# The input projection in seven block products instead of eight, in two causal halves

## The chip, the cores and the metric

The kernel runs on one core of a Trainium2 chip, in fp32 throughout. The metric is the device time of one execution in microseconds (us), lower is better. TensorE (PE) does the matrix products, VectorE (DVE) and ScalarE (ACT) the elementwise work, SyncE (SP) issues nearly all DMAs. A matmul writes to PSUM, of which there are eight banks of 128 x 512 fp32.

## The reference

One step of a hybrid decoder layer, for 2048 prompt tokens and 8 single sample tokens, model width 1024. The input projection has 11,264 columns: three attention groups (q, k, v of 512 columns each; dilations 1, 4, 16), an attention gate, the HGRN q, f, i and gate (1024 each), and two merge gates (1024 each).

```python
h = rms_norm(x, norm_w)
q, k, v = [cols(h, w_in, base + j * ATT_W, ATT_W) ...]      # three groups
o, lse = dilated_attn_prompt(q, k, v, win, dil, slopes[g])  # 129 keys a query
att = sum_g softmax_g(lse) * o ;  att = att * silu(cols(h, w_in, OFF_ATT_GATE, ATT_W))
ho, s_new = hgrn2_chunked(hq, hk, hi, logf, s0)             # causal, a state per head
ho = rms_norm(ho, hg_norm_w) * silu(cols(h, w_in, OFF_HG_GATE, HG_VW))
merged = ga * (att @ w_att_proj) + gb * (ho @ w_hg_proj)
y = x + merged @ w_out                                      # then a final rms_norm
```

The sample tokens attend to three caches of keys and values (8 heads of 64, 8 sequences) and update a stored HGRN state of 8 sequences x 8 heads x 128 x 128. Keys, values and states are outputs too.

## The kernel before

**Products.** The normalized input stays in SBUF, transposed, split into a high and a low fp32r part (`hh`, `hl`), in five token chunks of 512, 512, 512, 256 and 264 (the last holds the 8 sample tokens). A weight block is split the same way. A product takes three passes: high x high, high x low, low x high. `nat` makes 128 tokens x 256 columns (V of attention, i of HGRN) with 24 matmuls of 256 columns. `proj_T` makes 128 columns x all tokens, with the weights as the stationary side: per column block and chunk 24 matmuls, at L320, L321 and L322. Each chunk has a PSUM tile of its own (`pp`, two or three banks in rotation), so an eviction lies beside the next chunk's matmuls.

**Stages**, in the order of TensorE: `nat_block` over ten column blocks; attention, 12 pairs of a head pair j and a group g, where the projection of one pair stands beside the scores, the transposes of the probabilities and the value products of the pair before (`att_proj`, `att_side`); `combine` with the decode attention (`samp_score`, `samp_softmax`, `samp_av`) and gates between; HGRN, eight heads, with the projections of f, q and gate and merge gates; the sample HGRN (`samp_hg`, L891 to L905, and `samp_hg_end`) with merge gates between the heads; a branch `tc.If` (L977) that an exact version is behind; the last merge gate; and the final products. Scores of attention go through VectorE (bias and row maximum), ScalarE (exponential), TensorE (transposes) and a copy, block after block.

**What sets the order.** The kernel's code is put in order by a scheduler with priorities: `tc.high_priority` raises weight loads and splits. Every engine executes its queue in order. Pools of buffers decide how early a load may start.

The lines that make one product, as they stand before:

```python
for t0, npr, n in chunks:
    ci = chunk_of(t0)[0]
    ps = ps_proj()
    for k in range(KT):
        TE.matmul(ps[:, 0:n], hi[:, k], hh[ci][:, k], start=(k == 0), stop=False)
        TE.matmul(ps[:, 0:n], hi[:, k], hl[ci][:, k], start=False, stop=False)
        TE.matmul(ps[:, 0:n], lo[:, k], hh[ci][:, k], start=False, stop=(k == KT - 1))
    evac(ci, t0, npr, ps)
```

## Time and profile before

| | before |
|---|---|
| time, median of 3 runs | 3129.62 us (3129.3 to 3129.8) |
| span of the profiled execution | 3129.9 us |
| PE busy | 3077.8 us, 98% |
| DVE busy | 1215.5 us, 39% |
| ACT busy | 1090.5 us, 35% |
| matmuls | 19836 |
| DMA | 282.89 MB, mean 90 GB/s |

Busy time is the time in which an engine has an instruction under way. Matmuls overlap, and their ends are modelled, so that a TensorE that is held up a little between two matmuls still counts as busy. Start-to-start times of equal matmuls show the rate. Where a stage is looked at, its length, the work in it and the granted clock stand in one row of the windows view.

### The profile page before, as it was taken

The numbers are of one execution on the slowest core, as the hardware profiler recorded it, in microseconds if no ns is written. First come the engines' busy times: TensorE is split into PE (matmuls) and PEld (weight loads), VectorE is DVE, ScalarE is ACT, GpSimd is POOL, SyncE is SP. The second block draws the span as 40 slices with busy tenths as digits, with TensorE's granted clock in tenths as the row PEclk, the third lists the DMA queues.
The fourth block names the chain that finished last, engine by engine and source line by source line (L and its number), as shares of the span: only waits on it lengthen the run. The fifth ranks groups of instructions, "written<-read, shape, count | busy, mean of one in ns | idle before, by whom it ended". The sixth has DMA issues, their size and how long they took to land. (4 is left out here: it accounts for less than half of the span.)

```text
span 3129.9 us, 49890 instructions
## 1 busy us (share of the span) xinstructions
PE 3077.8 (98%) x19836; PEld 2607.1 (83%) x19836; DVE 1215.5 (39%) x3445; ACT 1090.5 (35%) x2506; POOL 3.1 (0%) x9
## 2 busy tenths in 40 slices
PE   8999999999999999999999999999999989899999
PEld 8999999777777777777878688888888868899987
DVE  5311110332332332333665055555555523634443
ACT  4311110333333333335333166655555431311231
POOL 0000000000000000000000000000000000000000
PEclk9999999999999999999999999999999989999999
DMA  5323211111111111111784311111111263744542
GB/s 167 98 89 105 79 58 41 43 45 55 42 45 55 43 45 56 42 45 64 231 275 157 121 50 42 45 41 44 40 49 48 69 183 116 223 143 134 158 149 80
DMA packets 326244, 282.89 MB, mean 90 GB/s; under 512 B 21161, under 2 KB 284026, under 8 KB 325474
## 3 DMA queue, kind: packets, MB, share of 16 engines
q1 hardware_dynamic: 325378, 277.72, 28.6%
q8 instruction: 157, 2.57, 0.3%
q0 software_dynamic: 336, 1.05, 0.1%
q10 hardware_dynamic: 288, 0.85, 0.1%
q14 instruction: 85, 0.70, 0.1%
HBM read 179.12 MB, written 100.94 MB: 89 GB/s over the span
## 5 line engine op out<-in xcount | busy, mean ns | idle before, releaser
L320 PE MATMUL pp<-hh,wh 128*128 128x512 f32 (+2 forms) x2680 | 956.6, 357 | 5.1 <-ACT gm L526 4.4
L321 PE MATMUL pp<-hl,wh 128*128 128x512 f32 (+2 forms) x2680 | 947.6, 354 | 0.0
L322 PE MATMUL pp<-hh,wl 128*128 128x512 f32 (+2 forms) x2680 | 946.6, 353 | 0.0
L320 PEld LDWEIGHTS pp<-hh,wh 128*128 128x128 f32 x2680 | 506.6, 189 | 86.2 <-issue 9.9
L321 PEld LDWEIGHTS pp<-hl,wh 128*128 128x128 f32 x2680 | 507.7, 189 | 73.0 <-issue 8.3
L322 PEld LDWEIGHTS pp<-hh,wl 128*128 128x128 f32 x2680 | 505.5, 189 | 75.0 <-issue 7.9
L207 PE MATMUL pp<-wnh,hh 128*128 128x256 f32 x1296 | 369.7, 285 | 0.5 <-ACT hh L232 0.5
L209 PE MATMUL pp<-wnh,hl 128*128 128x256 f32 x1296 | 367.5, 284 | 0.0
L208 PE MATMUL pp<-wnl,hh 128*128 128x256 f32 x1296 | 367.4, 283 | 0.0
L207 PEld LDWEIGHTS pp<-wnh,hh 128*128 128x128 f32 x1296 | 247.6, 191 | 4.8 <-issue 3.5
L209 PEld LDWEIGHTS pp<-wnh,hl 128*128 128x128 f32 x1296 | 247.5, 191 | 0.7 <-DVE hl L235 0.2
L208 PEld LDWEIGHTS pp<-wnl,hh 128*128 128x128 f32 x1296 | 247.6, 191 | 0.4
L415 ACT ACTIVATE sc<-sc,stg 128x256 f32<-128x256 f32 (+1 forms) x384 | 175.6, 458 | 115.7 <-DVE stg L413 115.5
L176 ACT ACTIVATE wh<-wr 128x512 fp32r<-128x512 f32 x134 | 77.4, 624 | 360.3 <-PE pp L321 356.7
L413 DVE CUSTOM_DVE_ANT_0 sc<-px,bt 128x256 f32<-128x256 f32 (+1 forms) x384 | 131.0, 364 | 176.1 <-PE px L411 146.4
L177 DVE TENSOR_TENSOR wl<-wr,wh 128x512 fp32r<-128x512 f32 x134 | 86.8, 688 | 220.8 <-ACT wh L176 219.9
L411 PE MATMUL px<-kT,qT 64*128 64x256 f32 (+1 forms) x768 | 164.7, 379 | 0.0
L264 DVE COPY vst<-pp 128x256 f32<-128x256 f32 x80 | 33.9, 424 | 281.7 <-PE pp L209 281.6
L264 ACT COPY vst<-pp 128x256 f32<-128x256 f32 x80 | 29.7, 372 | 320.7 <-PE pp L209 302.1
L423 PEld LDWEIGHTS px<-cm,sc 128*128 128x128 f32 x600 | 66.0, 140 | 85.4 <-ACT sc L415 38.6
L423 PE MATMUL px<-cm,sc 128*128 128x128 f32 x600 | 130.4, 297 | 6.1 <-ACT sc L415 5.7
L176 ACT ACTIVATE th<-ra 128x256 fp32r<-128x256 f32 (+1 forms) x148 | 57.9, 417 | 221.8 <-PE pp L1025 156.9
(363 smaller groups left out, 4405.8 us busy)
## 6 DMA issues: line engine op xcount, KB each, us to landing
wr<-in_w_in SPq DMA_DIRECT2D x136, 256.0 KB
natt<-stg SPq DMA_DIRECT2D x48, 264.0 KB
na<-natt SPq DMA_DIRECT2D x48, 264.0 KB
vscr<-vst SPq DMA_DIRECT2D x48, 256.0 KB
vt<-vscr SPq DMA_DIRECT2D x48, 256.0 KB
g<-gm SPq DMA_DIRECT2D x45, 256.0 KB
wnr<-in_w_in SPq DMA_DIRECT2D x40, 256.0 KB
xt<-in_x_prompt SPq DMA_DIRECT2D x16, 512.0 KB
```

Source lines behind the costliest of these rows:

```text
L176: A.activation(out=hi, in_=raw, func=AF.Copy)
L177: V.tensor_tensor(out=lo, in0=raw, in1=hi.bitcast(F32), op=ALU.subtract)
L207: TE.matmul(ps[0:m, 0:256], lhs_hi[:, k], wt[0][:, k], start=(k == 0), stop=False)
L208: TE.matmul(ps[0:m, 0:256], lhs_hi[:, k], wt[1][:, k], start=False, stop=False)
L209: TE.matmul(ps[0:m, 0:256], lhs_lo[:, k], wt[0][:, k], start=False, stop=(k == KT - 1))
L320: TE.matmul(ps[:, 0:n], hi[:, k], hh[ci][:, k], start=(k == 0), stop=False)
L321: TE.matmul(ps[:, 0:n], hi[:, k], hl[ci][:, k], start=False, stop=False)
L322: TE.matmul(ps[:, 0:n], lo[:, k], hh[ci][:, k], start=False, stop=(k == KT - 1))
L411: TE.matmul(spss[hx][:, 0:W], qT[hs, blk * P:(blk + 1) * P], kT[hs, k0:k0 + W], start=True, stop=True)
L413: V.tensor_tensor_reduce(out=sc[:, hx, 0:W], in0=spss[hx][:, 0:W], in1=bt[:, hx, 256 - W:256], scale=1.0, scalar=3e38, op0=ALU.add, op1=AL ...
L415: A.activation(out=sc[:, hx, 0:W], in_=sc[:, hx, 0:W], func=AF.Exp, scale=-1.0, bias=stg[:, u, 128 + hx:129 + hx], accum_out=stg[:, u, 130 ...
L423: TE.transpose(pt[:, hx * W + w * P:hx * W + (w + 1) * P], sc[:, hx, w * P:(w + 1) * P], ident)
```

## The change

One level of Strassen's scheme (in Winograd's form) on the input projection. A product of 1024 tokens (a causal half p) with a pair of column blocks is split in two along the contraction (512 + 512), the tokens (r = 0, 1; 512 each) and the pair. Seven block products, in the order `A11, A12, S2, S3, S1, A22, S4`, take the place of eight; each still has three passes.

- `make_H` makes the seven combinations of the input, each split in high and low, for one half of the tokens; there is one set of tiles, written again for the second half (`hscr` keeps the normalized input meanwhile).
- `w_combos` makes the seven of the weights, per pair and half, with eleven operations of VectorE and seven of ScalarE.
- `t_pair` (the matmuls at L362, L364, L365) replaces `proj_T`: three accumulators `pa`, `pb`, `pc`, one bank each; `pa` is reused four times a chunk after a copy by ScalarE (`keep_c`), `pc` twice. The chunks of a block are 256 and 260 tokens in the first half (with four sample tokens) and 512 in the second (`SETS`).
- `nat_block` (L308, L310, L311) does the same with two banks each.
- Natural products, attention, combine and HGRN run for the first half, then for the second; keys go through DRAM (`kscr`), the HGRN state stays in SBUF (`carry_s`). Dilation 16 works on 64-row pieces.
- The decode attention stands in the first half's combine stage. The sample HGRN stands between the halves, without projections between its heads. The flag is read and the branch taken after the second half, and one merge pair stands behind the branch.

```diff
+HALF = T // 2
+SW = 512 + NS // 2
+SETS = (((0, 256), (256, 260)), ((0, 512),))
+ORDER = ("A11", "A12", "S2", "S3", "S1", "A22", "S4")
...
+    def make_H(a11, a12, a21, a22, cs):
+        def put_h(s, src):
+            split_w(src, Hh[s][:, :, cs], Hl[s][:, :, cs])
+
+        put_h("A11", a11)
+        put_h("A12", a12)
+        V.tensor_tensor(out=a11, in0=a11, in1=a21, op=ALU.subtract)
+        V.tensor_tensor(out=a21, in0=a21, in1=a22, op=ALU.add)
+        put_h("A22", a22)
+        V.tensor_tensor(out=a22, in0=a22, in1=a11, op=ALU.subtract)
+        put_h("S2", a22)
+        put_h("S3", a11)
+        put_h("S1", a21)
+        V.tensor_tensor(out=a12, in0=a12, in1=a22, op=ALU.subtract)
+        put_h("S4", a12)
...
+            def prod(ps, i, ks, first=False):
+                hi, lo = Hh[ORDER[i]], Hl[ORDER[i]]
+                wh, wl = W[i]
+                o = ps[:, 0:n]
+                for k in ks:
+                    TE.matmul(o, wh[:, k], hi[:, k, off:off + n], start=(first and k == 0), stop=False,
+                              skip_group_check=True)
+                    TE.matmul(o, wh[:, k], lo[:, k, off:off + n], start=False, stop=False, skip_group_check=True)
+                    TE.matmul(o, wl[:, k], hi[:, k, off:off + n], start=False, stop=(k == 3), skip_group_check=True)
+
+            def keep_c(ps):
+                c = pl.tile([P, 512], F32, name="cc", tag=cc[0], bufs=cc[1])
+                A.copy(out=c[:, 0:n], in_=ps[:, 0:n])
+                return c
...
+            pa, pb = ps_proj(0), ps_proj(1)
+            prod(pa, 0, k4, True)
+            c1 = keep_c(pa)
+            prod(pb, 1, k4[:2], True)
+            prod(pa, 2, k4)
+            c2 = keep_c(pa)
+            prod(pb, 1, k4[2:])
+            fin(0, 0, pb, c1)
+            prod(pa, 3, k4)
+            c3 = keep_c(pa)
+            pc = ps_proj(2)
+            prod(pc, 4, k4, True)
+            fin(1, 1, pc, c3)
+            prod(pa, 5, k4)
+            fin(1, 0, pa, None)
+            prod(pc, 6, k4)
+            fin(0, 1, pc, c2)
...
+    att_stage(0)
+    cb_stage(0)
+    hg_stage(0)
...
+        merge_pair(mp, 0, 4)
+        merge_pair(mp, 0, 6)
+        alloc_H()
+        with tc.high_priority(HP):
+            make_H(hraw[0, 0], hraw[0, 1], hraw[1, 0], hraw[1, 1], slice(0, 512))
+    with pool("mg") as mp:
...
+        merge_pair(mp, 1, 0)
...
+        for h in range(8):
+            samp_hg(h)
+        samp_hg_end()
```

The sample HGRN on TensorE. Before, the products of a late head (L902) stand among the matmuls of a merge gate:

```order
L902 MATMUL px<-sv,qss 32x128
L321 MATMUL pp<-hl_130,wh 128x512
L902 MATMUL px<-sv,qss 32x128
L322 MATMUL pp<-hh_129,wl 128x512
L902 MATMUL px<-sv,qss 32x128
L320 MATMUL pp<-hh_129,wh 128x512
L902 MATMUL px<-sv,qss 32x128
```

In the changed kernel, at the end of the merge pair and ahead of the natural products (L308 to L311) of the second half:

```order
L362 MATMUL pc<-hhS_16269,wh 128x512
L364 MATMUL pc<-hlS_16270,wh 128x512
L365 MATMUL pc<-hhS_16269,wl 128x512
L1058 MATMUL px<-sv,qss 32x128 x64
L1075 MATMUL px<-cm,on 128x128 x16
L308 MATMUL pa<-wh,hhA_16257 128x256 x2
L310 MATMUL pa<-wl,hhA_16257 128x256
L311 MATMUL pa<-wh,hlA_16258 128x256
```

All 64 products of the sample state and the 16 transposes behind them moved into one piece between two stages.

SyncE behind the branch, where `ra` are the inputs of the final products and `rr` their weights, before:

```order
L977 UNCONDITIONAL_BRANCH
L965 DMA ra<-att_86 128x256
L965 DMA ra<-att_87 128x256
L965 DMA ra<-att_88 128x256
L965 DMA ra<-att_89 128x256
L965 DMA ra<-ho 128x256 x8
L995 DMA rr<-in_w_att_proj 128x4x128
```

and after, with `wr` the weights of the last merge pair:

```order
L1221 UNCONDITIONAL_BRANCH
L1211 DMA ra<-att_106 128x256
L1211 DMA ra<-att_107 128x256
L1211 DMA ra<-att_108 128x256
L1211 DMA ra<-att_109 128x256
L1211 DMA ra<-ho 128x256 x8
L212 DMA wr<-in_w_in 128x4x128 x4
L1238 DMA rr<-in_w_att_proj 128x4x128
```

The four weight loads of the last pair now stand behind the twelve loads of the final stage; before, the last gate's weights were loaded ahead of the branch.

## Rows read from the trace of the kernel before

**Rows 1.** The page, busy us of each engine and share of the span.
```profile
PE 3077.8 (98%) x19836; PEld 2607.1 (83%) x19836; DVE 1215.5 (39%) x3445; ACT 1090.5 (35%) x2506; POOL 3.1 (0%) x9
```

**Rows 2.** Windows by stage: length, busy us (instructions) per engine, clock, DMA.
```profile
0.00:505.00 505.00, 493.48 (x4153) 485.04 (x4154) 124.15 (x266) 101.03 (x220) 0.20 (x4) 1.00 0.30 96
505.00:1500.00 995.00, 988.47 (x6046) 738.89 (x6045) 296.45 (x1100) 355.80 (x1076) 0.00 (x0) 1.00 0.17 51
1500.00:1800.00 300.00, 294.04 (x1556) 236.86 (x1556) 151.92 (x393) 87.45 (x133) 0.00 (x0) 0.99 0.59 192
1800.00:2485.00 685.00, 685.00 (x4136) 600.49 (x4134) 381.19 (x1052) 396.51 (x700) 0.00 (x0) 1.00 0.14 44
2485.00:2660.00 175.00, 161.97 (x937) 131.83 (x936) 51.05 (x133) 45.70 (x116) 2.86 (x5) 0.94 0.53 153
```

**Rows 3.** Timeline of PE: start, us, then the instruction; first and last of runs.
```profile
511.62 0.39 PE L321 MATMUL pp<-hl,wh 128*128 128x512 f32 x1
...
521.65 0.39 PE L322 MATMUL pp<-hh,wl 128*128 128x512 f32 x1
...
522.01 0.28 PE L321 MATMUL pp<-hl,wh 128*128 128x256 f32 x1
...
524.50 0.28 PE L322 MATMUL pp<-hh,wl 128*128 128x256 f32 x1
...
443.48 0.28 PE L209 MATMUL pp<-wnh,hl 128*128 128x256 f32 x1
...
446.96 0.28 PE L208 MATMUL pp<-wnl,hh 128*128 128x256 f32 x1
```

**Rows 4.** Windows by stage, line L320 alone: PE busy (matmuls), weight loads, clock, DMA.
```profile
505.00:1500.00 995.00, 382.65 (x1067) 201.61 (x1067) 1.00 0.17 51
1500.00:1800.00 300.00, 164.69 (x463) 87.76 (x464) 0.99 0.59 192
1800.00:2485.00 685.00, 339.47 (x957) 180.15 (x957) 1.00 0.14 44
2485.00:2660.00 175.00, 84.31 (x235) 45.03 (x234) 0.94 0.53 153
```

**Rows 5.** Timeline of PE in attention: the output transposes of two neighbouring groups of blocks.
```profile
562.65 0.60 PE L442 MATMUL px<-cm,ot 128*128 128x128 f32 x4
...
574.17 0.60 PE L442 MATMUL px<-cm,ot 128*128 128x128 f32 x4
```

**Rows 6.** Timelines of the start: VectorE's operations of 512 columns, the first product.
```profile
11.54 1.29 DVE L177 TENSOR_TENSOR wnl<-wnr,wnh 128x512 fp32r<-128x512 f32 x2
...
13.48 0.58 PE L207 MATMUL pp<-wnh,hh 128*128 128x256 f32 x1 [0.50 <-ACT hh L232]
```

**Rows 7.** Windows: the 50 us with the most DMA.
```profile
1550.00:1600.00 50.00, 47.05 (x244) 39.78 (x243) 37.08 (x92) 17.11 (x25) 0.00 (x0) 0.97 0.83 266
```

**Rows 8.** Timeline of ScalarE: the eviction of a 256-column chunk.
```profile
524.82 0.39 ACT L347 ACTIVATE qT<-pp 128x256 f32<-128x256 f32 x1 [2.13 <-PE pp L322]
```

**Rows 9.** Lines: the most frequent table load of ScalarE, busy us, mean ns.
```profile
L672 ACT ACT_TABLE_LOAD x32 | 41.1, 1283 | 0.6
```

**Rows 10.** Timelines of SyncE, ScalarE and VectorE in the sample HGRN.
```profile
2561.72 0.38 SPq L893 DMA_DIRECT2D sv<-in_state_hgrn  x1
...
2568.62 0.38 SPq L905 DMA_DIRECT2D out<-sv  x1
...
2596.24 4.81 SPq L927 DMA_DIRECT2D ho<-ots  x8
...
2565.77 2.44 ACT L898 ACTIVATE sv<-sv,fs 128x128 f32<-128x128 f32 x8 [2.66 <-DMA sv<-in_state_hgrn]
...
2578.01 2.40 DVE L899 SCALAR_TENSOR_TENSOR sv<-ib,kss,sv 128x128 f32<-128x128 f32 x8 [9.41 <-ACT sv L898]
```

**Rows 11.** Timeline of SyncE behind the branch.
```profile
2626.88 1.75 SPq L965 DMA_DIRECT2D ra<-att  x4
2628.67 4.69 SPq L965 DMA_DIRECT2D ra<-ho  x8
```

**Rows 12.** Waits of PE: the last merge gate for the branch, us, times, longest.
```profile
PE pp L320 <- ACTq L977: 3.6, 1, 3.6
```

More of the change, by code (lines that the diff above doesn't have):

```diff
@@ L862, in hg_exact @@
[L862 to L863 removed]
+                    TE.matmul(ps, pt1, u, start=True, stop=True)
+                    V.tensor_tensor(out=o, in0=o, in1=ps, op=ALU.add)
+                proj(bass.ds(h * P + OFF_HG, P), ev_silu(1.0))
+                V.tensor_tensor(out=u, in0=o, in1=o, op=ALU.mult)
                 ps = ps_side()
[L865 removed]
@@ L866, in hg_exact @@
[L866 to L871 removed]
+                TE.matmul(ps, ones, u, start=True, stop=True)
@@ L927, in samp_hg_end, with att_stage @@
                 sto(ho_scr[h][:, T:TT], ots[:, h])
-        merge_gate(mp, *merge_list.pop(0))
-        samp_hg_prep()
+        return samp_hg_prep, samp_hg, samp_hg_end
+    def att_stage(p):
+        with pool("at") as at:
+            pend = None
+            for j in range(4):
+                for g in range(3):
+                    nxt = (p, j, g) + att_proj(at, p, j, g) if pend is None else None
+                    if pend is not None:
+                        att_side(at, *pend)
+                        nxt = (p, j, g) + att_proj(at, p, j, g)
+                    pend = nxt
+            att_side(at, *pend)
@@ L931, in body @@
+    with banks(6, ABC), pool("wn") as wn:
+        for g, half in ((0, 0), (1, 0), (2, 0), (3, 0), (3, 1)):
+            nat_block(wn, 1, g, half)
+    bk = banks(3, ABC)
+    bk.__enter__()
+    open_T(5, 5)
+    att_stage(1)
+    cb_stage(1)
+    hg_stage(1)
+    with pool("fl") as mp:
         f1 = mp.tile([P, 1], F32, name="f1")
```

1079 lines of the change are left out of this document (606 added, 473 removed).

## The prediction

> **What bounds the kernel now.** I read the page first: TensorE is busy 98% of the span [rows 1]. The windows by stage come next [rows 2]: the granted clock is 1.00 except around the sample state, VectorE and ScalarE are at most 58% busy in any stage, so no other engine is the bound of a stage as a whole. A busy TensorE is not one at its peak, so I took start-to-start times: 43 matmuls of 512 columns in 10.03 us, 0.2333 us each; 22 of 256 columns in 2.49 us, 0.113; 29 of the natural-layout ones in 3.48 us, 0.120 [rows 3]. The 264-column form I scale from the 256-column one, 0.117 us. One column block of `proj_T` is then 72 x 0.2333 + 24 x 0.113 + 24 x 0.117 = 22.3 us. The count of L320 in a stage over 40 gives its column blocks [rows 4]: 26.7, 11.6, 23.9 and 5.9. What a stage takes beyond its projection is the rest that the change has to live with:
>
> - natural-layout stage: 505 - 3840 x 0.120 = 44 us
> - attention: 995 - 26.7 x 22.3 = 400
> - combine and decode attention: 300 - 259 = 41
> - HGRN heads: 685 - 533 = 152
> - sample HGRN and merge gates: 175 - 132 = 43
>
> The final stage, 470 us, is not touched. The kernel is bound by products in most places, and by chains in attention, where four blocks take 11.52 us from one output transpose to the next [rows 5].
>
> **What the change removes.** Seven block products for eight. Transposed side: before, 68 x 22.3 = 1516 us. After, 34 pairs x 84 x (0.113 + 0.115) = 651 us in the first half (chunks of 256 and 260) and 34 x 84 x 0.2333 = 666 us in the second (512): 1317, or **-199**. Natural side: 3840 to 3360 matmuls at 0.120: **-58**. Sum -257 us, 8.2%. The matmul counts in the order of the changed kernel bear this out, so the change does on TensorE what it says. The columns of one instruction hardly matter (0.113 against 0.2333/2), so the short chunks cost nothing by themselves.
>
> **What it adds.**
>
> *Start, +16 (10 to 30).* All seven combinations of the first half have to exist before the third product: four token pairs, each four normalizing operations and twelve of 512 columns for VectorE, at 1.29 us for two [rows 6], that is some 4 x 10 us, and the first weights' eleven double-size operations beside them, some 12. TensorE has only two products (96 matmuls, 12 us) to do meanwhile. I put the third product at 53 us, where before the stream runs from 13.48 us on [rows 6]. That would idle some 37 us, of which a stage rest of 44 already holds the old start, its transposes and the sample rows.
>
> *Attention, +43 (10 to 155).* Dilation 16 in 64-row pieces: twice the small products for four of the twelve groups, +13. The other chains are the same blocks, cut into halves. Four times 11.52 us is 46 us a side, 553 for twelve, against a rest of 400: projection matmuls now cover 153 of it. If this cover were lost wholly, +155; if kept, 0. With 39 us of projection a group instead of 44.6, and twice as many starts, I take a fifth, +30.
>
> *Combine and decode attention, +48 (5 to 75).* All of the decode caches is now read in the first half's stage, beside four pairs of projection, 4 x 19.2 = 77 us. The loads there are 24 each of key rows, query rows, attention results and value rows at about 0.26 MB, with gates, results and weights some 38 MB. The busiest 50 us of the trace moved 266 GB/s [rows 7], so 38 MB take 143 us, 25 MB (if only decode counts) 93. The matmuls over the value rows stand together behind the softmax with hardly a projection between them. I take 150 us for this stage and 92 for its second half: rests of 73 + 16 = 89 against 41.
>
> *HGRN, +45 (0 to 100).* Each accumulator now has one bank. An eviction's round trip: last 256-column matmul starts 524.50 [rows 3], ScalarE begins at 524.82 and takes 0.39 [rows 8], 0.71 us, against half a product, six matmuls or 0.68 us, put in between: the 256-column chunks have no slack, the 512-column ones some. ScalarE executes in order, and a table load takes 1.283 us [rows 9]; behind one, with its operation, a copy comes about 2 us late. Three such reuses in each of 48 chunks are exposed; one late in each is 48 x 2.1 = 100 us, none is 0. The rows that would say which end is nearer do not exist: the stage before has two or three free banks. I take the middle. Sixteen halves of a head last 48 us of TensorE by rate (39 projection, 9 side); VectorE needs some 39 of them by the row durations of its operations and ScalarE 35, more than the 56 and 58% of before [rows 2].
>
> *Sample HGRN, second set of H, and the end, +55 (35 to 75).* Before, the eight heads interleave with merge gates and TensorE idles 13 of 175 us [rows 2]. Now its 64 matmuls stand in one piece behind a merge pair and ahead of the second half's natural stage. Two state buffers: a load is 4.05 us from issue to ScalarE's first use (2561.72 to 2565.77), a head 2.44 us there, the store follows [rows 10]; two heads take about 11.7 us, and six of eight come after the pair: 35 us. From VectorE's last update, 2578.01 + 2.40, to the store of the result, 2596.24, is 16 us, and that store's eight issues take 4.81 [rows 10]. On SyncE the new weights stand behind these: 4.05 and a split of 1 more. TensorE idles some 62 us; waiting for the second H (the last five combinations can only be written once the old ones are read) adds 5. At the end the flag, the branch, then the twelve loads of the merge inputs, 6.5 us [rows 11], stand ahead of the last pair's weights on SyncE: 6.5 + 4 + 2 and the flag's 5, some 18 us where 3.6 were waited [rows 12]. 62 + 5 + 18 + some 13 of matmuls = 98 against 43.
>
> *Others, +8:* two more stage borders, with pools that close and open.
>
> **Where the skill speaks against it.** In the trace TensorE's rest of 400 us in attention left the clock at 1.00 [rows 2]. The Trainium skill, TensorE: Matmul & The Clock Gate, section "A second HAM failure mode: psum-queue depth-cycling", says that cycling through PSUM banks can make TensorE idle so briefly and so often that its clock falls and rises again between bursts. The trace of before, with pauses of the same kind in attention, does not agree. The same skill, Perfetto Trace Analysis, section "Matmuls", asks independent matmul groups to rotate through PSUM banks so that one's eviction lies beside the next one's products; by it the HGRN term would be at its upper end and the sum 55 us later; no run here shows it yet.
>
> **Sum.** -257 + 16 + 43 + 48 + 45 + 55 + 8 = -42. The profiled span is 3129.9 us, the median of the runs 3129.6, so the difference can be set against either: 3088 us. With rounding of the rests I say **3090 us**, 1.3% faster. A measurement of this kernel tells about 0.2% (6 us) from no change.
>
> **Rivals.**
> 1. *Nearly all is kept.* The scheduler fills chains and loads as well as before: all terms at their low ends, 10 + 10 + 5 + 0 + 35 = 60, 2930 to 3030 us. For it: 42% of the engines' time is free in HGRN. Against: the two serial pieces stand in the order and need no luck. 0.16.
> 2. *Slower: HGRN waits in order.* VectorE and ScalarE run at three quarters of each half of a head, and in-order queues with one bank a product turn each late table load into TensorE waiting. Without its HGRN term the sum is -87; so from 87/16 = 5.4 us a half of a head the kernel gets slower. At 8 us it is 128, and 3171; with attention's cover going the same way up to 3260. For it: the round trip of 0.71 against 0.68. Against: the 512-column half has twice the cover, 1.4 us. 0.32.
> 3. *Even.* The sample state's chain and the cache loads both come out slow, at their upper ends (75 and 75 instead of 55 and 48), all else as forecast: -42 + 47 = +5, 3135; even is 3124 to 3136. For it: both pieces stand together in the order. Against: two upper ends at once. 0.07.
> 4. *The clock.* If one-bank waiting made the clock fall for a third of HGRN and attention after, at half rate: their 28 pairs of each half, 56 x 19.4 = 1086 us, a third of it again: +360, 3450. Before, 0.94 was granted only around the idle of the sample stage [rows 2]. This is what the first rule above would do. 0.03.
>
> My forecast, part of the gain kept (3030 to 3123), has 0.42; its own range is 3035 to 3123. Faster is 0.42 + 0.16 = 0.58, even 0.07, slower 0.32 + 0.03 = 0.35. The range that holds 8 in 10 leaves out the top of rival 2 with rival 4, and the bottom of rival 1: 2970 to 3215 us.
>
> **What would show it.** In the profile after: 512- and 256-column matmuls still 0.233 and 0.113 us apart, natural stages 0.120; TensorE idle about 62 us ahead of the second natural stage with the clock low there; some 18 us ahead of the last merge pair; a DMA rate above 220 GB/s in the first combine stage with TensorE waiting for value rows; the third product at 50 to 55 us; HGRN halves of 51 us. The forecast is wrong if HGRN halves last above 54 us, or if attention takes more than 950 us over both halves (24 pairs of 19.4 and a rest of 443 are 909).

## The result, and the profile after

The changed kernel takes 3269.1 us (median of 4 runs, 3264.5 to 3269.8) against 3129.7 before: 1.044 times, 95% interval 1.043 to 1.046. It is slower by 139 us where 40 us faster was forecast. The page of the profiled execution, busy time of each engine as in [rows 1]:

```profile
span 3268.0 us, 54030 instructions
PE 2930.1 (90%) x20260; PEld 2514.7 (77%) x20260; DVE 1882.2 (58%) x4622; ACT 1474.3 (45%) x3276; POOL 2.5 (0%) x8
```

TensorE's busy time fell by 148 us, and the time that it isn't busy rose from 52 to 338 us. No other engine came above 58%. The windows by stage, with the columns of [rows 2]; the stages now run in this order: natural, attention, combine with decode, HGRN of the first half; merge pairs with the sample HGRN; the same four of the second half (natural to HGRN); the end; the final stage:

```profile
0.00:314.00 314.00, 250.35 (x1977) 234.91 (x1977) 156.07 (x255) 120.06 (x208) 0.20 (x4) 0.89 0.37 120
314.00:757.00 443.00, 434.31 (x3692) 365.80 (x3692) 233.17 (x744) 211.60 (x653) 0.00 (x0) 0.99 0.26 74
757.00:945.00 188.00, 140.75 (x854) 114.01 (x852) 133.38 (x336) 63.54 (x121) 0.00 (x0) 0.85 0.68 207
945.00:1400.00 455.00, 417.48 (x3288) 403.59 (x3288) 332.11 (x903) 288.09 (x611) 0.00 (x0) 0.97 0.23 70
1400.00:1575.00 175.00, 79.65 (x481) 63.87 (x479) 72.28 (x131) 58.68 (x130) 0.00 (x0) 0.70 0.48 117
1575.00:1785.00 210.00, 204.42 (x1688) 203.21 (x1688) 89.11 (x90) 58.77 (x77) 0.00 (x0) 0.97 0.36 120
1785.00:2245.00 460.00, 449.80 (x2846) 320.36 (x2845) 247.21 (x676) 228.22 (x624) 0.00 (x0) 1.00 0.29 84
2245.00:2340.00 95.00, 87.51 (x374) 66.66 (x373) 80.17 (x202) 47.03 (x74) 0.00 (x0) 0.98 0.61 191
2340.00:2738.00 398.00, 373.60 (x1866) 298.34 (x1865) 297.70 (x713) 281.32 (x498) 0.00 (x0) 1.00 0.22 66
2738.00:2786.00 48.00, 26.35 (x108) 20.72 (x107) 21.74 (x50) 11.22 (x18) 1.76 (x3) 0.75 0.41 121
2786.00:3268.00 482.00, 465.88 (x3105) 423.27 (x3103) 219.23 (x523) 105.73 (x266) 0.54 (x1) 0.99 0.51 150
```

The reader is to take a stage's length and subtract its projection by the rates of the prediction (19.2 or 19.6 us a pair, 0.120 us a natural-layout matmul), which gives the rests that the prediction spoke of:

| part | projection | rest before | rest after | change | forecast (bounds) |
|---|---|---|---|---|---|
| natural, 314 + 210 us | 403 | 44 | 121 | +77 | +16 (10 to 30) |
| attention, 443 + 460 | 24 pairs, 466 | 400 | 437 | +37 | +43 (10 to 155) |
| combine, 188 + 95 | 8 pairs, 155 | 41 | 128 | +87 | +48 (5 to 75) |
| HGRN, 455 + 398 | 32 pairs, 620 | 152 | 233 | +81 | +45 (0 to 100) |
| middle and end, 175 + 48 | 4 pairs, 78 | 33 | 145 | +112 | +55 (35 to 75) |
| final | - | 480 | 482 | +2 | 0 |

(The final stage before starts at 2650, so 10 us of the last window of [rows 2] are its own, and 33 stands for the 43 of the prediction.) With -257 for the products these make +139; the spans differ by 138. The gain in products came; the rests took it back and more. How much of each change is idle time of TensorE can be read from the rows, as length less PE busy: natural 12 to 69 us, attention 7 to 19, combine 6 to 55, HGRN 0 to 62, middle and end 13 to 117. The remainder of each change is TensorE busy for longer, with side work, at a lower granted clock or at the rates below.

The rates of the forecast were a little low for the short chunks. Twelve matmuls of 256 columns from 1009.91 to 1011.22 are 0.119 us apart; the medians of the first HGRN stage are 0.118 (256 columns) and 0.120 (260), those of the second 0.232 (512), of the natural stages 0.118. A pair of the first half takes 20.0 us by these and not 19.2, some 27 us over 34 pairs, which stand in the rests of the table.

Where TensorE waited longest in the span (engine, line, what it waited for; us in total, times, longest):

```profile
PE pa L362 <- ACT cc L369: 62.2, 56, 5.2
PE px L1058 <- DVE sv L1055: 52.5, 8, 8.6
PE pb L362 <- DVE cc L409: 22.2, 6, 14.3
PE pa L308 <- ACT wh L189: 21.3, 3, 9.0
PE px L256 <- DVE xt L251: 19.4, 4, 11.1
PE pp L362 <- ACT wh L189: 19.0, 1, 19.0
```

The first is the snapshot, and no wait of before is like it: the change keeps a running sum of products in one bank (P0, then P0+P2, then P0+P2+P3), and ScalarE copies it out (line 369) before the next product may be added. The second is the sample state, the third mostly the second half's combinations of H, the fourth and sixth the first weights of a block or pair, the fifth the normalizing of the start. Of the fifth, 11.1 us are the very first token tile, which the kernel before waits for as well; it also has one wait of 7.7 us for the sample state.

```profile
PE px L230 <- DVE xt L225: 11.0, 1, 11.0
```

ScalarE and TensorE around one late snapshot, in the first HGRN stage (start, us, instruction):

```profile
1017.30 1.28 ACT L814 ACT_TABLE_LOAD   x1
1018.60 0.81 ACT L814 ACTIVATE qt<-qt,lb,omlb 128x512 f32<-128x512 f32 x1
1019.43 1.28 ACT L842 ACT_TABLE_LOAD   x1
1020.73 0.63 ACT L842 ACTIVATE tk<-qt 128x512 f32<-128x512 f32 x1
1021.26 0.35 ACT L369 COPY cc<-pa 128x256 f32<-128x256 f32 x1
```
```profile
1009.91 0.28 PE L362 MATMUL pb<-hhA,wh 128*128 128x256 f32 x1
...
1018.68 0.28 PE L365 MATMUL pa<-hhA,wl 128*128 128x256 f32 x1
1021.67 0.58 PE L362 MATMUL pa<-hhS,wh 128*128 128x256 f32 x1 [2.71 <-ACT cc L369]
```

The bank's last product ends at 1018.96, and the copy starts 2.3 us later: ScalarE takes its work in order, and Ln, a table load and Exp stand ahead of the copy.

The source puts six matmuls of `pb` between these two products of `pa`. In TensorE's queue there are none: the scheduler had moved the pair's twelve matmuls of `pb` forward, and they ran from 1009.91 on. Counted in the timeline of seven half-heads (967 to 1373), 21 of 85 snapshots have no projection matmul between them and the next product into the bank, and these hold 22.3 of the 23.5 us that TensorE waited for snapshots there; 2.7 us come once in every half-head, at this place.

### The profile page after: what moved, and what is told of

It reads as the page before. It is cut to its first block, busy times and chain, and to the rows that moved or that the text cites. A ratio compares the mean times of both kernels' runs of the same rounds, so it can differ in the third digit from the quotient of the medians.

```text
span 3268.0 us, 54030 instructions
## 1 busy us (share of the span) xinstructions
PE 2930.1 (90%) x20260; PEld 2514.7 (77%) x20260; DVE 1882.2 (58%) x4622; ACT 1474.3 (45%) x3276; POOL 2.5 (0%) x8
## 5 line engine op out<-in xcount | busy, mean ns | idle before, releaser
L189 ACT ACTIVATE wh<-wr 128x512 fp32r<-128x512 f32 (+1 forms) x546 | 364.2, 682 | 606.0 <-PE pa L364 275.2
L190 DVE TENSOR_TENSOR wl<-wr,wh 128x512 fp32r<-128x512 f32 (+1 forms) x546 | 405.3, 756 | 311.3 <-ACT wh L189 293.1
L362 PE MATMUL pa<-hhS,wh 128*128 128x256 f32 (+2 forms) x808 | 280.6, 347 | 44.8 <-ACT cc L369 42.6
L362 PE MATMUL pa<-hhA,wh 128*128 128x256 f32 (+2 forms) x808 | 274.7, 340 | 40.1 <-ACT cc L369 19.5
L362 PE MATMUL pc<-hhS,wh 128*128 128x256 f32 (+2 forms) x808 | 262.1, 324 | 15.2 <-DVE cc L409 15.2
L364 PE MATMUL pa<-hlS,wh 128*128 128x256 f32 (+2 forms) x808 | 267.8, 331 | 0.0
L365 PE MATMUL pa<-hhS,wl 128*128 128x256 f32 (+2 forms) x808 | 267.5, 331 | 0.2 <-DVE wl L190 0.2
L364 PE MATMUL pa<-hlA,wh 128*128 128x256 f32 (+2 forms) x808 | 266.3, 330 | 0.0
L365 PE MATMUL pa<-hhA,wl 128*128 128x256 f32 (+2 forms) x808 | 265.6, 329 | 0.0
L365 PE MATMUL pc<-hhS,wl 128*128 128x256 f32 (+2 forms) x808 | 261.3, 323 | 0.0
L364 PE MATMUL pc<-hlS,wh 128*128 128x256 f32 (+2 forms) x808 | 260.5, 322 | 0.0
L362 PEld LDWEIGHTS pa<-hhS,wh 128*128 128x128 f32 x808 | 156.6, 194 | 82.0 <-ACT cc L369 63.9
L362 PEld LDWEIGHTS pa<-hhA,wh 128*128 128x128 f32 x808 | 156.9, 194 | 64.6 <-ACT cc L369 30.9
L362 PEld LDWEIGHTS pc<-hhS,wh 128*128 128x128 f32 x808 | 155.8, 193 | 30.4 <-issue 12.6
L365 PEld LDWEIGHTS pa<-hhA,wl 128*128 128x128 f32 x808 | 157.1, 194 | 13.1 <-issue 1.2
L364 PEld LDWEIGHTS pa<-hlA,wh 128*128 128x128 f32 x808 | 157.3, 195 | 10.7 <-issue 1.0
L365 PEld LDWEIGHTS pa<-hhS,wl 128*128 128x128 f32 x808 | 156.5, 194 | 11.5 <-issue 1.4
L364 PEld LDWEIGHTS pa<-hlS,wh 128*128 128x128 f32 x808 | 156.5, 194 | 10.1 <-issue 1.5
L364 PEld LDWEIGHTS pc<-hlS,wh 128*128 128x128 f32 x808 | 155.2, 192 | 11.7
```

Source lines behind the costliest of these rows:

```text
L189: A.activation(out=hi, in_=raw, func=AF.Copy)
L190: V.tensor_tensor(out=lo, in0=raw, in1=hi.bitcast(F32), op=ALU.subtract)
L362: TE.matmul(o, wh[:, k], hi[:, k, off:off + n], start=(first and k == 0), stop=False, skip_group_check=True)
L364: TE.matmul(o, wh[:, k], lo[:, k, off:off + n], start=False, stop=False, skip_group_check=True)
L365: TE.matmul(o, wl[:, k], hi[:, k, off:off + n], start=False, stop=(k == 3), skip_group_check=True)
```

## The experiments

A half-head is one head of HGRN in one half of the tokens; a stage has eight. Cover is the TensorE work that stands between a snapshot and the next product into the same bank.

Theory A: the rests grew because pieces of work stand in a row, on engines whose queues keep order, with no projection beside them (start, decode, sample state, second H, end). Theory B: the running sum leaves too few matmuls between a snapshot and its next product. Theory C: VectorE and ScalarE are the bound of the stages with 256-column chunks, so that moving work helps nothing. Theory D: the snapshot is late because of what stands ahead of it in ScalarE's queue, the table loads above all. A ratio is against the kernel before, which took 3130.8 to 3131.6 us beside the runs; "gain" is against the 3269 of the changed kernel.

### Pieces that stand in a row

**The sample state between the combines of the second half** instead of in the middle.
```diff
                 combine(cb, j, (2 * p, 2 * p + 1))
+                if p == 1:
+                    samp_hg(2 * j)
+                    samp_hg(2 * j + 1)
```


> The eight sample-state heads and their end are taken out of the piece between the halves and stand two by two in the second half's combine stage (which has room for their buffers), beside its four pairs of projection. Theory A (the products are saved as forecast, 257 us; the time is lost in serial pieces between the stages): TensorE's waits for the sample state (52.5 + 8.3 us) and some clock loss go, the combine stage grows by 10 to 20 us as VectorE is 84% busy there: 40 to 65 us less than the changed kernel's 3269, 3205 to 3230. Rival B (the loss is in the snapshots of the running sum, in every pair): the serial piece is only moved, under 20 us less, above 3250. Rival C (VectorE's doubled work is the bound): the work in the combine stage costs what it saved, 3260 to 3280.

Measured: 3233.8 us, ratio 1.033 (1.031 to 1.034), a gain of 35, a little less than theory A's 40 to 65. The stretch from the end of the first HGRN to the second natural stage fell from 202 to 116 us, but the second combine rose from 102 to 151. ScalarE's and TensorE's waits there:
```profile
ACT sv L1062 <- DMA sv<-in_state_hgrn: 23.3, 8, 4.8
```
```profile
PE pa L362 <- ACT cc L369: 17.5, 7, 6.2
```
ScalarE waits for the state's loads, and the snapshots stand behind it: in the kernel changed the second combine has no wait for a snapshot. A serial piece that is moved takes its queue with it: a little over half of the 86 us were paid again.

**The decode attention beside the second half's natural blocks.**
```diff
-                if p == 0:
-                    for _ in range(6):
-                        samp_score(*scores.pop(0))
...
             nat_block(wn, 1, g, half)
+            if i < 3:
+                for _ in range(8):
+                    samp_score(*scores.pop(0))
```


> The whole decode attention stands beside the natural products of the second half instead of in the first half's combine stage. Theory A: the first combine stage shrinks from 188 to about 95 us (as the second one), the natural stage grows from 205 to at most 230: 65 to 90 us less than 3269, 3180 to 3205. Rival B: the combine stage's length is that of its eight chunks' snapshots, 10 to 20 us less. Rival C (VectorE is the bound): some 40 us less, the 33 us of multiplying and summing cached rows and their waits, since VectorE is only 42% busy in the natural stage.

Measured: 3228.4, ratio 1.031 (1.029 to 1.032), a gain of 41. That is what rival C named (some 40), not theory A's 65 to 90. From the last value product of the first attention to the first scores of HGRN the time fell from 246 to 174 us (721.3 to 967.2, and 718.7 to 892.7); the second natural stage rose by 17 and the start of attention behind it by 16, where the softmax ends. TensorE's waits in the first combine stage of the kernel changed say the same:
```profile
PE pa L362 <- ACT cc L369: 10.4, 16, 2.4
PE pb L362 <- DVE cc L409: 7.8, 4, 2.4
PE pc L362 <- DVE cc L409: 5.5, 2, 3.0
PE px L749 <- DMA vc<-in_cache_kv_w: 4.9, 7, 2.7
```
With three smaller ones (5.4, 5.4 and 4.1 us) the waits for VectorE are 28 us, those for the cached value rows 4.9. VectorE is busy for 133 of the 188 us, 33 of them with the cached rows.

**The second H in four pieces of 128 tokens.**
```diff
-            make_H(hraw[0, 0], hraw[0, 1], hraw[1, 0], hraw[1, 1], slice(0, 512))
+        for u in range(4):
+            us = slice(u * P, (u + 1) * P)
+            make_H(*[hraw[r, k][:, :, us] for r in range(2) for k in range(2)], us)
```


> The second set of input combinations is made in four pieces of 128 tokens at ordinary priority instead of one piece of 512 at high priority. Theory A: the additions that TensorE waits for (14.3 + 11.4 us) get between the pieces: 10 to 25 us less, 3245 to 3260. Against it: all seven tiles are still only free once the last pair of the first half has read them, and finer pieces cost VectorE and ScalarE 0.1 us each: 0 or some us more. Rivals B and C: no change, within 8 us of 3269.

Measured: 3265.8, ratio 1.043 (1.041 to 1.044), no gain beyond the spread: the wait of 14.3 us became this one.
```profile
PE pa L364 <- DVE hlA L190: 17.3, 1, 17.3
```
VectorE in the kernel changed, around the wait of 14.3:
```profile
1431.86 4.49 DVE L190 TENSOR_TENSOR hlA<-hr,hhA 128x2048 fp32r<-128x2048 f32 x2 [0.39 <-ACT hhA L189]
...
1453.86 2.28 DVE L190 TENSOR_TENSOR hlS<-hr,hhS 128x2048 fp32r<-128x2048 f32 x1
...
1457.34 0.41 DVE L409 TENSOR_TENSOR cc<-pb,cc 128x256 f32<-128x256 f32 x1
```
From the first row to the last it stands still for only 0.3 of 25.5 us, with the combinations of H and the splits of weights, and the eviction that TensorE waits for stands behind them. Here, as in the first combine, theory C holds: VectorE's rate, not the grain, is the bound.

**Four of these additions on GpSimd.**
```diff
-        V.tensor_tensor(out=a11, in0=a11, in1=a21, op=ALU.subtract)
+        E.tensor_tensor(out=a11, in0=a11, in1=a21, op=ALU.subtract)
```


> The four additions of the second set of input combinations go from VectorE to GpSimd. Theory E (at this place VectorE's rate is the bound: twelve operations of 2.29 us stand one behind the other from the release of the first tile on): 9 us of VectorE go, TensorE's wait of 14.3 us gets shorter by some 6, if GpSimd takes no more than 4 us for one; 3260. If GpSimd takes 6 us or more for one, the time grows by 5 to 15 us.

Measured: 3281.4, ratio 1.048 (1.047 to 1.050), 12 slower. GpSimd's first and last addition, and VectorE beside the first two:
```profile
1432.10 6.52 POOL L199 TENSOR_TENSOR hr<-hr,hr 128x2048 f32<-128x2048 f32 x1 [1431.64 <-DVE hlA L190]
...
1462.69 4.51 POOL L206 TENSOR_TENSOR hr<-hr,hr 128x2048 f32<-128x2048 f32 x1
```
```profile
1434.13 10.54 DVE L190 TENSOR_TENSOR wl<-wr,wh 128x512 fp32r<-128x512 f32 x3
```
Each addition takes two to three times VectorE's 2.29 us. And VectorE was not freed: two of its three splits of 128x512 beside GpSimd's first two additions took 5.04 and 4.98 us, the third, behind them, 0.68; in the kernel changed one takes 0.69.

**The start**: three load buffers instead of two, the first weights at high priority, and the second half's token tiles two by two behind the later natural blocks instead of all eight behind the first.
```diff
-            for tt in range(8, 16):
-                st = x_tile(tt)
...
+            for i, (g, half) in enumerate(((1, 0), (2, 0), (3, 0), (3, 1))):
+                nat_block(wn, 0, g, half, hs)
+                for tt in (8 + 2 * i, 9 + 2 * i):
+                    st = x_tile(tt)
```


> The first token tiles have three load buffers instead of two (three result buffers instead of four), the first block's weight combinations are raised in priority, and the second half's eight token tiles are normalized two by two behind the four other natural blocks instead of all behind the first. Theory A: the start's loss is a chain of loads and of tiles in SyncE's and ScalarE's order, so 30 to 50 us less, 3220 to 3240. Rivals B and C: VectorE's work at the start is the same; up to 10 us less.

Measured: 3233.1, ratio 1.033 (1.031 to 1.034), a gain of 36, as expected: the natural stage ends at 262 us instead of 303. The third product before the edit and behind it:
```profile
72.73 0.80 PE L308 MATMUL pa<-wh,hhS 128*128 128x256 f32 x2 [6.96 <-ACT wh L189]
```
```profile
63.80 0.50 PE L312 MATMUL pa<-wh,hhS 128*128 128x256 f32 x2 [0.96 <-ACT wh L189]
```
So 9 of the 36 us are the third product's. Most of the rest goes with the normalizing of eight tiles in one piece, a thing that the prediction had not seen: between 90 and 200 us TensorE waited 21 us in the kernel changed, and behind 80 us only 0.4 in the natural stage of this run. The edit's three parts were not run apart.

### The snapshots

**Nine, nine and six matmuls of cover instead of six, six and twelve** in the source: the same products, taken in other portions.
```diff
-            prod(pb, 1, k4[:2], True)
+            prod(pb, 1, k4[:3], True)
             prod(pa, 2, k4)
             c2 = keep_c(pa)
-            prod(pb, 1, k4[2:])
+            prod(pb, 1, k4[3:])
             fin(0, 0, pb, c1)
+            prod(pc, 4, k4[:2], True)
             prod(pa, 3, k4)
```


> The matmuls between a snapshot of the running sum and the next product into it are spread as 9, 9 and 6 instead of 6, 6 and 12. Theory A: the exposed round trips at 256 columns (0.71 us against 0.68) gain half an interval of cover each, some 0.3 us in two of three snapshots of 96 chunks: 10 to 30 us less, 3240 to 3260. Rival B (snapshots are the main loss): 50 to 100 us less, 3170 to 3220. Rival C: no change.

Measured: 3268.6, ratio 1.044 (1.043 to 1.046), no gain. Seven half-heads of HGRN last 406.2 us against 405.9; the waits below are 25.7 us against 23.5. At the place of the row above, six matmuls now stand in between where there were none, and TensorE waits 2.18 us instead of 2.71; other places got short waits instead. Against a copy that starts 2.5 us late, six matmuls (0.7 us) are too few, so this speaks for theory D and doesn't settle theory B.

**Chunks of 512 columns in the first half.** The sample columns of the transposed projection are left out, with a constant in their place.
```diff
-SETS = (((0, 256), (256, 260)), ((0, 512),))
+SETS = (((0, 512),), ((0, 512),))
```


> Leaves out the sample tokens' columns of the transposed projection (a constant stands for them), so that a block of the first half is one chunk of 512 columns as in the second half: half as many snapshots, each with twice the cover (six matmuls of 0.233 instead of 0.113 us). Theory A (as it stands after the first runs: serial pieces, and in-order queues of ScalarE and VectorE in HGRN): the first half's HGRN stage goes from 58 to 53 us a head as in the second half, 40 us, attention and combine give 5 to 20: 45 to 60 us less than 3269, 3205 to 3225. Rival B (round trip of the snapshots): 100 us less or more, as the 28 pairs of attention and HGRN each gain 3 us or more. Rival C (VectorE): 20 us less, for the fixed part of its smaller operations.

Measured: 3180.4, ratio 1.016 (1.015 to 1.018), a gain of 89, between theory A's 45 to 60 and rival B's 100: by the source the same number of matmuls lies between snapshots, each twice as long, and half as many snapshots are taken. The wait for snapshots fell from 62.2 to 33.4 us in the whole span. Some 15 us of the gain go with the rate (34 pairs at 19.5 instead of 20.0 us), and the samples' evictions are left out too.

**One table for all.** The exact functions of HGRN and the gates (Sigmoid, Ln, Exp, Sqrt) are left out, with copies in their place.
```diff
-                    A.activation(out=qt[r][:, off:off + npr], in_=z, func=AF.Sigmoid)
+                    A.activation(out=qt[r][:, off:off + npr], in_=z, func=AF.Copy)
```


> Leaves out the exact functions in the HGRN stages: sigmoid, exponential, logarithm and root are replaced by copies with scale and offset, so that ScalarE loads no function tables there (31 of 172 loads are left, 141 x 1.283 = 181 us of ScalarE). Theory A: snapshots stand behind table loads in ScalarE's queue; HGRN goes from 58 and 53 us a head to 52 and 50: 60 to 80 us less, 3190 to 3210. Rival B (round trip alone): 20 us less, since the round trip stays. Rival C (VectorE is the bound, 74% busy there): under 15 us less.

Measured: 3201.1, ratio 1.023 (1.021 to 1.024), a gain of 68, in theory A's range (60 to 80) and above those of rivals B and C. It comes from both halves: seven half-heads take 377 us instead of 406 in the first and 342 instead of 374 in the second.

**Both left out** (the two edits above).

> Leaves out both the sample columns of the transposed projection and the functions of HGRN (as in the two runs before). If the two causes are one and the same waits (theory D: the snapshot stands behind other work in ScalarE's queue; fewer snapshots or less work ahead of them both end it), the first half's HGRN goes no lower than TensorE's own 48 to 49 us a head, and the sum is less than 89 + 68: 120 to 135 us less than 3269, 3135 to 3150. If they are apart (a fixed price of a chunk, a fixed price of a table), the sum is full: 157 us less, 3112.

Measured: 3129.6, ratio 0.9996 (0.999 to 1.001), a gain of 140, between the two forecasts (120 to 135, and the full sum of 157). Chunks of 512 act in the first half alone, so there the two can be compared: seven half-heads of HGRN gain 48 us by the chunks, 29 by the table and 61 by both (the rows below). Of the 29, 16 are the same time.

**Two running sums.** The two chunks of the first half go side by side, each with a sum and a bank of its own, so that a product of the other chunk lies between a snapshot and the next product. Nothing is left out.
```diff
+        for b in range(2):
+            prod(pa[b], b, 2, k4)
+            c2[b] = keep_c(pa[b], b)
...
-    bk = banks(3, ABC)
+    bk = banks(4, ABCD)
```


> In the first half the two chunks of a block go side by side, each with a running sum and a bank of its own, so that 24 matmuls (2.7 us) stand between a snapshot and the next product into the same sum instead of 6 or 12; the number of snapshots and additions stays, and the side work has four banks instead of five. Cover theory (the snapshots of small chunks come too late, whatever makes them late): HGRN of the first half goes from 58 us a head to 50 to 52, attention and combine as with chunks of 512: 60 to 85 us less than 3269, 3185 to 3210. Count theory (the number of evictions and additions on ScalarE and VectorE is what costs): under 15 us less. If four side banks are too few, HGRN or attention get longer, 3270 or more.

Measured: 3206.8, ratio 1.025 (1.023 to 1.026), a gain of 62. Seven half-heads of the first HGRN stage, in the kernel changed, with chunks of 512, with one table, with both, and with two running sums (columns of [rows 2]):
```profile
967.00:1373.00 406.00, 373.49 (x2962) 361.35 (x2961) 300.73 (x821) 260.08 (x558) 0.00 (x0) 0.98 0.22 65
```
```profile
947.00:1305.00 358.00, 348.17 (x1779) 286.40 (x1779) 278.06 (x660) 261.72 (x455) 0.00 (x0) 1.00 0.24 73
```
```profile
957.00:1334.00 377.00, 368.82 (x2976) 355.57 (x2976) 296.96 (x828) 198.87 (x510) 0.00 (x0) 1.00 0.24 70
```
```profile
941.00:1286.00 345.00, 343.71 (x1766) 285.50 (x1765) 275.18 (x661) 186.18 (x391) 0.00 (x0) 1.00 0.25 75
```
```profile
943.00:1313.00 370.00, 359.30 (x2954) 351.66 (x2953) 291.74 (x825) 273.39 (x572) 0.00 (x0) 1.00 0.24 71
```
Two running sums give back 36 of these 406 us while VectorE and ScalarE work about as long as before (292 and 273 us for 301 and 260): theory C falls for HGRN. In the whole span the wait for snapshots fell from 62.2 to 24.6 us, 38 of the gain of 62. TensorE's waits for snapshots in the same stretches, in the kernel changed, with the 9, 9 and 6 of cover, with one table and with two running sums:
```profile
PE pa L362 <- ACT cc L369: 23.5, 15, 2.7
```
```profile
PE pa L362 <- ACT cc L369: 25.7, 30, 2.2
```
```profile
PE pa L362 <- ACT cc L369: 3.1, 8, 1.6
```
```profile
PE pa L363 <- ACT cc L374: 9.3, 7, 2.3
```
With one table, and the cover unchanged, the wait goes from 23.5 to 3.1: it is made of table loads ahead of the copy (theory D). With two sums 24 matmuls stand in between by the source, 2.8 us, more than the copy is late, and the wait falls too (B). They are two ends of one wait.

**Samples by small products of their own**, to have chunks of 512 with nothing left out.
```diff
+                        for kk in range(4):
+                            TE.matmul(ps[32 * kk:32 * kk + 32, c * P:(c + 1) * P], hs32[:, 4 * r + kk], rw[r, c][:, kk],
+                                      start=(r == 0 and c == 0), stop=(r == 1), skip_group_check=True)
```


> Nothing is left out: the eight sample tokens are projected by products of their own in the first half (sixteen fp32 matmuls of 128 columns a pair, the sample tokens stationary, then two small products that add and transpose), and the block is one chunk of 512 columns. The changed kernel's sample rows of the natural stage take 0.06 to 0.12 us each, so the addition is 1 to 2 us a pair, 35 to 70 us. With chunks as the cause (theory D, after run e5: what the 256-column chunks cost, 89 us, is ScalarE's and VectorE's queue in which each snapshot stands): 3180 + 35 to 70, 3215 to 3250. If the small products wait for weights on TensorE's queue, above 3250.

Measured: 3300.3, ratio 1.054 (1.052 to 1.056), 31 slower, and 120 slower than the chunks of 512 alone, 3.5 us for each of 34 pairs where 1 to 2 were expected. The samples' products need the raw weights, which the combinations then overwrite; the wait for a pair's first weights over the whole span is
```profile
PE pa L383 <- ACT wh L195: 22.8, 22, 5.3
```
where the kernel changed has 11.5, so late weights are a small part. In the first attention (314 to 761 us, and 314 to 713 with chunks of 512 alone) the granted clock was 0.94 and not 1.00, and TensorE was busy for 428 us and not 392. How the 120 us divide stays open.

### Together

**The start, decode in the second natural stage, and the sample state in half-heads inside the second HGRN stage** with its updates on VectorE, and the last pair's weights ahead.
```diff
             for h in range(8):
                 t = hg_fq(h)
+                if p == 1:
+                    samp_hg(h, 0)
                 hg_decay(h, *t)
...
                 hg_gate(h, t[3], ss)
+                if p == 1:
+                    samp_hg(h, 1)
```


> The start of the run before, the decode attention beside the second half's natural products, the sample state half a head at a time in the second half's HGRN stage with a shorter end (the norm's sum over channels is a product with ones), and the last pair's weights raised to the priority of the loads ahead of it. Theory A: 40 (start) + 41 (decode, as measured) + 70 (sample state with its end, less 10 for the work in HGRN) + 5: 140 to 160 us less, 3110 to 3130, about the time before the change. Rival B: 80 us less. Rival C: the sample state's work on VectorE makes HGRN of the second half longer by all it takes, 30 us: 3150.

Measured: 3140.7, ratio 1.003 (1.002 to 1.005), a gain of 128 where 140 to 160 were expected. Most of theory A bears out: with no product's arithmetic changed, moving pieces gives back 128 of the 139 us. But the part that rival C named came as well: the sample state made seven half-heads of the second HGRN stage 32 us longer, 406 us (2203 to 2609) where the kernel changed has 374 (2354 to 2728).

Samples by their own products on top of it (the edit shown with that run):

> The combined version with the sample tokens' own products and chunks of 512. From 3141: chunks of 512 give 75 to 89, the small products cost 35 to 70: 3085 to 3135, so at most 1.5% faster than the kernel before the change. If the addition stands in TensorE's queue at the wrong place, 3150.

Measured: 3161.0, ratio 1.009 (1.008 to 1.011): 20 slower than without. Instead of that, **each sigmoid as a tanh** (the halves folded into constants), and one Ln for 1024 columns:
```diff
-                    A.activation(out=qt[r][:, off:off + npr], in_=z, func=AF.Sigmoid)
+                    A.activation(out=qt[r][:, off:off + npr], in_=z, func=AF.Tanh, scale=0.5)
```


> The combined version of 3141 us with the sigmoids as hyperbolic tangents, exact in value (halves and ones are folded into operations that are there), since ScalarE keeps that function and the exponential in one table, and one logarithm of 1024 columns instead of two: some 85 table loads instead of 172. If the late snapshots stand behind table loads, half of the 68 us of run e6 and a little in the combine stages: 25 to 45 us less, 3095 to 3115. If ScalarE's order changes for the worse or the wider VectorE forms (0.665 against 0.605 us) decide, 3130 to 3145.

Measured: 3089.0, ratio 0.987 (0.985 to 0.989): 52 less than without, and 1.3% faster than before. In seven half-heads of HGRN 28 table loads are left of 50 (counted in the version below); 15 of these 22 go with the tanh, 7 with the one Ln. Last, **the two running sums as well** (their edit as shown above):

> The combined version with the tangents and the two running sums. Cover theory: the two causes are mostly the same waits in the first half, so 3141 less 25 to 45 less 40 to 70: 3030 to 3080, which would be faster than the kernel before the change by 1.5 to 3%. Count theory: as the run before, within 10 us.

Measured: 3015.4, ratio 0.963 (0.961 to 0.965), 114 us faster than the kernel before, with nothing left out. Its page:
```profile
span 3017.9 us, 53848 instructions
PE 2859.1 (95%) x20262; PEld 2474.2 (82%) x20262; DVE 1873.2 (62%) x4725; ACT 1337.5 (44%) x3099; POOL 2.5 (0%) x8
```
and its two longest waits of TensorE:
```profile
PE pb L375 <- DVE cc L457: 25.0, 12, 15.3
PE pp L375 <- ACT wh L198: 12.7, 1, 12.7
```
No wait for a snapshot is among its seven longest; the second H (15.3 of the 25.0) and the last weights are left. Of the 254 us between this and the changed kernel, 128 came from the pieces in a row (A), 52 from the tables (D) and 74 from the second sum (B), in this order; alone, the second sum gave 62. The tanh was not tried on the kernel before; in its HGRN stage TensorE was busy for 685.0 of 685 us [rows 2], so it had no wait of TensorE to take away there.

## Why the prediction was wrong

The saving was right; what failed is the sum of what the change adds. Three terms were too small (the start by 61 us, combine by 39, the middle and the end by 57), each a piece worked out by the rate of its loads or of one engine, with nothing for the work of other engines that it stands behind. In HGRN (36 too small) the overlap was wrong: six matmuls were counted between a snapshot and the next product, and TensorE's queue has none where it waits longest.

- **What the change removes, -257.** Right. TensorE does the forecast's products, and with the medians of both traces (before, 0.117 and 0.121 us for 256 and 264 columns, where one chunk gave 0.113) the saving is 254. But the short chunks cost 0.5 us a pair more than one of 512, where the prediction put nothing. The final version is faster by 114 us, so a good part of the gain can be kept.
- **"Start, +16 (10 to 30)"** measured +77, a miss of 61. The third product came at 72.7 us, not 53. The term took VectorE's operations as the bound, but VectorE was busy for 32 of the first 50 us and 35 of the next 50: TensorE waits by turns for tiles, for ScalarE's splits and for the first weights (7.0 us just ahead of the third product). And the eight tiles of the second half, which the prediction put at nothing, stand in one piece behind the first natural block. The run of the start gave 36 back; what the other 25 are stays open. The granted clock was 0.89 in that stage.
- **"Attention, +43"** measured +37. The number is right, the mechanism only in part: lost cover was to be most of it, but TensorE's idle time grew by 12 us alone, and some 10 are the rate of the short chunks.
- **"Combine and decode attention, +48 (5 to 75)"** measured +87. The loads were taken by rate, 143 us for 38 MB, and the chain of decode was put beside them. The length of the first stage was 188 us against the 150 forecast, but not by the loads: 207 GB/s were moved, and TensorE waited for value rows for 4.9 us, for VectorE for 28 and for snapshots for 10.4 of the 47 us in which it was idle. What the term had at nothing is VectorE, busy with the cached rows and with the evictions in one queue. Decode elsewhere is worth 41. The granted clock was 0.85; what that cost isn't told apart. (The rest of the second half's stage, 16 in the forecast's sum, is 13.6 by its own 19.6 us a pair.)
- **"HGRN, +45: I take the middle"** measured +81, within its bounds. A half-head lasted 58.0 us in the first half and 53.4 in the second, where 51 was said and 54 named as the limit. The mechanism named, a copy behind a table load on ScalarE, came, and at about its price: the waits for snapshots in the two stages are 27.7 + 12.0 = 40 us. But it came in another way, once or twice in a half-head and not now and then in every chunk, because the scheduler had moved the cover away. What the term left out is 21 us of other waits, most of them for VectorE's reads of the accumulators (8.8) and for operands that ScalarE or VectorE make (8.2), and some 13 us of rate. Without table loads 61 us of the two stages' fourteen half-heads are gone, more than the waits for snapshots, so other waits go with them.
- **"Sample HGRN, second set of H, and the end, +55 (35 to 75)"** measured +112. The sample chain took 52.5 + 8.3 + 9.0 = 70 us of waits where 62 was said, the end 19.0 where 18 was: both about right. The second H cost a wait of 14.3 and, behind it, late snapshots of 11.4 in this stage where 5 was said: VectorE's eleven operations of 2.29 us had not been counted against its other work. The clock granted in the 50 us of the sample chain was 0.50 (the lower level, 1.2 GHz), and the products of the state took 0.42 us each there; in the run with the state in the second combine, at 0.80 to 0.94, half of them took less than 0.30. 70 + 19 + 26 is 115 of the 145; the other 30 are matmuls and what the clock cost, where 13 were said.

```profile
1500.00:1550.00 50.00, 13.40 (x80) 7.24 (x80) 11.98 (x40) 14.09 (x45) 0.00 (x0) 0.50 0.75 172
```

- **The rivals.** "Slower: HGRN waits in order" had 5.4 us a half-head as the point from which it decides; measured were 81 / 16 = 5.1, so by itself it would have made the kernel even. No rival came true as written. The nearest is the one given 0.07, both serial pieces at their upper ends: they went beyond these (112 and 87 where 75 was the end of each), and the start and HGRN went the same way. "Two upper ends at once" was no reason against it. Each of these terms is the time of a piece on one engine, worked out as if the engine and its queue were free, and as far as the waits show, the missing time is of one kind: what else stands in the in-order queues.
- **The clock.** The fourth rival didn't come: 0.97 or more in attention and HGRN. The Trainium skill, TensorE: Matmul & The Clock Gate, section "A second HAM failure mode: psum-queue depth-cycling", says that short and frequent idling between groups of matmuls can make the clock go down and up. The trace agrees in direction: the stretch with the snapshots has 0.98 where chunks of 512 have 1.00, by estimate some 8 of its 406 us. Attention before, which the prediction held against the rule, shows no such pauses: TensorE was busy for 988.47 of 995 us [rows 2]. The Trainium skill, Perfetto Trace Analysis, section "Matmuls", wants independent groups of matmuls to turn through PSUM banks. The run with a second, independent sum in a second bank agrees: it gave 62 us.

The Trainium skill, ScalarE: Activation LUTs, section "Table sets: the hidden batching unit", says that exp and tanh share a table set. The trace agrees: with tanh for sigmoid and one Ln for two, a half-head has four loads instead of seven, and none stands between a tanh and an Exp. Each load takes 1283 ns [rows 9].

## What to carry to other kernels

A scheme that saves products by adding reads of a running sum made TensorE wait here for whatever stood ahead of that read in another engine's queue: give it a second, independent sum, and take the table loads out of that queue, before counting the saving. Count the cover between a read and the next product in TensorE's queue as it was scheduled, not in the source. When a sequence is cut into halves, list every piece that now has no products beside it, and add what else stands in the queues that it needs; such terms are late together, so the range has to hold their upper ends at the same time. A piece that is moved to fill a hole takes its waits along: the sample state took half of its gain back in the second combine, and 32 us in HGRN even when cut into half-heads.

## What was not expected of the hardware

- An addition of 128x2048 fp32 took 2.29 us on VectorE and 4.5 to 6.5 on GpSimd; beside GpSimd's, VectorE's operations of 128x512 took 5.0 us instead of 0.69.
- TensorE's granted clock was 0.50 in the 50 us in which it was busy for 13.4 of them, and 0.85 in the first combine, at 75% busy, while attention, 98% busy, had 0.99 and 1.00.
- Of two edits to one wait the sum was not to be had: in seven half-heads of the first HGRN stage 48 and 29 us apart, 61 together.
